# Down projections: 12 of 22 blocks as 2x2 block products by 7 half-size products instead of 8

## The chip, the cores and the metric

One core of a Trainium2 chip runs one layer of a decoder. The metric is the device time of one execution in microseconds, the median of several runs. The engines are named as in the profile: PE is TensorE (its weight loads are PEld), DVE is VectorE, ACT is ScalarE, POOL is GpSimd, and SP is SyncE, whose queue (SPq) issues the loads.

## The reference, cut to what matters

```python
def swiglu(x, w_gate, w_up, w_down):
    return (jax.nn.silu(x @ w_gate) * (x @ w_up)) @ w_down

x = x + 0.5 * rmsnorm(swiglu(rmsnorm(x, pre), w_gate, w_up, w_down), post)   # first FFN
x = x + rmsnorm(hybrid_mixer(rmsnorm(x, pre), ...), post)                     # attention and mLSTM
x = x + 0.5 * rmsnorm(swiglu(rmsnorm(x, pre), w_gate, w_up, w_down), post)   # second FFN
```

There are 512 tokens, the model is 1024 wide and the FFN 2816 wide, all in float32. The change lies in the last product of each FFN: the activations (512 x 2816) times `w_down` (2816 x 1024), called the down projection. The first FFN is named `a` in the tiles, the second `b`.

## The kernel before, in words

Float32 products are made of three PE products. Each operand is split into a high part in the PE's own format (a cast on ACT) and a low part (the operand minus its high part, a subtraction on DVE). A product is high x high + low x high + high x low.

The activations lie in SBUF as `aT`, 22 blocks of 128 FFN rows by 512 tokens. The down projection takes one block after the other. For each, `load_w` loads 128 rows of `w_down` (512 KB) into one of three `wf` buffers and splits them into `wh`, `wl` (128x1024, five buffers each), and `get_x` splits the block of `aT` into `ah`, `al` (128x512, five buffers each). Then `step` adds 24 matmuls of 512 columns: four tiles of 128 tokens, two halves of the 1024 columns, three products. The eight sums fill the eight PSUM banks. The last four blocks (`KEEP`) are held back and done tile by tile, so that the norm of one tile of tokens runs beside the matmuls of the next.

Ahead of the down projection, `seven` makes the gate and up products, one unit per block of FFN rows, already as 2x2 block products by seven. A unit has seven products of 12 matmuls of 256 columns; its seventh (`finish`) is put into the next unit. The seventh of the last unit is put behind the first half of the first block of the down projection (`bridge`), so that PE has work while DVE and ACT finish the unit. `qa` and `qb` are its banks, `z`, `uv`, `s` its small results.

What sets the order: DVE, ACT, PE and the load queue each work through their own list in order, as a scheduler wrote it when the kernel was built. In `seven`, the class `Order` ties each DVE or ACT instruction behind the one before it, so there the list is the code's order. A load waits for the last reader of the buffer that it fills. For a `wf` buffer that is the subtraction on DVE that makes the low part.

Of the kernel before, what the change touches and what calls it, by code (L numbers as in the profile page):

```python
# [10 lines left out]
F32 = mybir.dt.float32  # L11
F32R = mybir.dt.float32r
# [4 lines left out]
P = 128  # L17
T = 512
NT = T // P
D = 1024  # L20
KD = D // P
FF = 2816
NF = FF // P
# [9 lines left out]
WMAX = 1024  # L33
# [6 lines left out]
def tile_hybrid_block(ctx: ExitStack, tc: tile.TileContext, a: dict):  # L40
    nc = tc.nc

    ids = ctx.enter_context(tc.tile_pool(name="ids", bufs=1))
    wpool = ctx.enter_context(tc.tile_pool(name="wpool", bufs=1))
    hpool = ctx.enter_context(tc.tile_pool(name="hpool", bufs=1))
    const = ctx.enter_context(tc.tile_pool(name="const", bufs=1, side="right"))
    act = ctx.enter_context(tc.tile_pool(name="act", bufs=1, side="right"))

    def new_pool(name, side="right"):
        return tc.tile_pool(name=name, bufs=1, side=side, reuse_waits="tile")  # L50

    class Work:
        pool = None
# [4 lines left out]
    work = Work()  # L58
# [6 lines left out]
    def pair(name):  # L65
        return [bank(f"{name}_{b}") for b in range(2)]
# [127 lines left out]
        hTl = hpool.tile([P, KD, T], F32R, tag="hTl", name=f"hTl_{name}")  # L194
        return hTh, hTl

    def down(pool, n, chunk_src, get_x, post, finish, todo, name, bridge=None):
        pins = []
        accs = [None] * NT
        held = []  # L200
        for kk in range(n):
            xh, xl = get_x(kk)
            wh, wl = load_w(chunk_src(kk), f"{name}d{kk}")
            if kk < n - KEEP:
                for t in range(NT):
                    if kk == 0:
                        accs[t] = pair(f"acc_{name}{t}")
                    for b in range(2):
                        step(accs[t][b], xh, xl, wh, wl, t, b, kk == 0, False)
                    if bridge and kk == 0 and t == 1:  # L210
                        bridge()
# [12 lines left out]

    def step(out, xh, xl, wh, wl, t, b, first, last):
        tk = slice(t * P, (t + 1) * P)
        cs = slice(b * 512, (b + 1) * 512)
        nc.tensor.matmul(out, lhsT=xh[:, tk], rhs=wh[:, cs], start=first, stop=False)  # L228
        nc.tensor.matmul(out, lhsT=xl[:, tk], rhs=wh[:, cs], start=False, stop=False)  # L229
        nc.tensor.matmul(out, lhsT=xh[:, tk], rhs=wl[:, cs], start=False, stop=last)  # L230

    def flush(todo):
        return todo.pop(0)() if todo else None
# [1 line left out]
    Q = KD // 2 * P  # L235
    H = T // 2
    ADD, SUB, MUL = ALU.add, ALU.subtract, ALU.mult
# [39 lines left out]
        part(4)  # L277
        return parts

    def seven(fs, wgu, x, low, scr, aT, name):  # L280
        do = Order()
# [76 lines left out]
        for i in range(len(fs)):  # L358
            u, v, w = us[i:i + 3]
            u.open()  # L360
            if prev:
                prev.inner()
                prev.silu(1)
            u.product(u.a, 1, True, False)
# [12 lines left out]
            if prev:  # L377
                prev.finish()
            if v:
                low4 = v.take((4,), v.gu[1][:, 1:2, :], 1)  # L380
                low4()
            u.product(u.a, 2, False, True)
            u.silu(0)
            if v:
                v.take((7, 5), v.ab)()
            u.product(u.b, 7, False, False)
            u.product(u.c, 3, False, True)
            if w:
                w.front()
            prev = u  # L390
# [3 lines left out]

    PLAIN = 4

    def ffn(pool, todo, first_w, hT, wgu, wd, post, finish, name, begin=None, pins=()):
        hTh, hTl = hT
        aT = pool.tile([P, NF, T], F32, name=f"aT_{name}")
        st = ExitStack()  # L400
        low = st.enter_context(new_pool(f"parts_{name}", "left"))
        scr = st.enter_context(new_pool(f"gu_{name}"))

        def close(f, pg):
            s = scr.tile([P, 2, H], F32, tag="s", bufs=1, name=f"s_{name}{f}").rearrange("p a b -> p (a b)")
            nc.scalar.activation(s, pg[0], AF.Silu)
            nc.vector.tensor_tensor(aT[:, f, :], pg[1], s, op=MUL)

        def load_plain(f):
            return [load_w(wgu[f, :, b * 1024:(b + 1) * 1024], f"{name}gu{f}{b}",  # L410
                           after=pins if f < EARLY and f + b else ()) for b in range(2)]

        early = []
        for f in range(EARLY):
            w = first_w if first_w and f == 0 else load_plain(f)
            early.append((*w, pair(f"pg_{name}{f}")))
        by_halves([(pg, (wg, wu)) for wg, wu, pg in early], hTh, hTl, todo)
        for f in range(EARLY):
            close(f, early[f][2])
        x = None  # L420
        for f in range(EARLY, PLAIN):
            w = load_plain(f)
            if f == EARLY:
                x = token_parts(low, aT[:, NF - 16:, :], hTh, hTl, name)
            pg = pair(f"pg_{name}{f}")
            for b in range(2):
                ws(pg[b], w[b], KD, hTh, hTl)
            close(f, pg)
        last = seven(range(PLAIN, NF), wgu, x, low, scr, aT, name)

        dn = ExitStack()
        dlow = []

        def bridge():
            last()
            st.close()
            dlow.append(dn.enter_context(new_pool(f"low_{name}", "left")))
            work.pool = dn.enter_context(new_pool(f"dn_{name}"))
            if begin:
                begin()  # L440


        def get_x(kk):
            if kk == 0:
                ah, al = (wpool.tile([P, WMAX], F32R, tag=f"w{y}", bufs=5, name=f"a{y}_{name}{kk}")[:, :T] for y in "hl")
            else:
                ah, al = (dlow[0].tile([P, T], F32R, tag=f"a{y}", bufs=5, name=f"a{y}_{name}{kk}") for y in "hl")
            nc.scalar.copy(ah, aT[:, kk, :])
            nc.vector.tensor_tensor(al, aT[:, kk, :], ah.bitcast(F32), op=ALU.subtract)
            return ah, al  # L450

        pins = down(pool, NF, lambda kk: wd[kk], get_x, post, finish, todo, name, bridge)
        dn.close()
        return pins


    with new_pool("ffn_a") as fa:
# [28 lines left out]
        hT = []  # L486
# [8 lines left out]
            todo.append(lambda: turn_norm(t, h, *hT, "mx"))  # L495

        op_ctx.close()
        pins = ffn(fa, todo, first_w, hT1, a["wgu1"], a["wd1"], post1, finish1, "a", begin=load_gains)
    hTh, hTl = hT


# [482 lines left out]
    pins = down(mg, KD, lambda kk: a["wout"][kk], lambda kk: (meTh[:, kk, :], meTl[:, kk, :]), post2, finish2, todo, "o")  # L984
    gctx.close()
    mctx.close()

# [2 lines left out]
    with new_pool("ffn_b") as fb:  # L990
        def post3(t):
            return PostNorm(t, g_post2[0], [(work, "tmp"), (work, "tmp2")][t % 2], "f2", True)

        def finish3(t):
            for c in BANKS:
                nc.sync.dma_start(a["out"][t * P:(t + 1) * P, c], xs[t][:, c])

        ffn(fb, todo, None, hT2, a["wgu2"], a["wd2"], post3, finish3, "b",
            begin=lambda: g_post2.append(gain(a["ffn2_post_g"], "f2post")), pins=pins)


# [29 lines left out]
def _layout(inp):  # L1031
# [10 lines left out]
    r = {"x": np.asarray(inp["x"])[0]}  # L1042
    for i, n in ((1, "ffn1"), (2, "ffn2")):
        r[f"wgu{i}"] = np.concatenate([cols(f(f"{n}_w_gate")), cols(f(f"{n}_w_up"))], 2)
        r[f"wd{i}"] = f(f"{n}_w_down").reshape(NF, P, D)
# [43 lines left out]
```

## Time and profile before

| | us |
|---|---|
| median of 3 runs | 1371.52 (1370.53 to 1372.25) |
| the profiled execution | 1370.57 |
| its span, first to last instruction | 1368.8 |
| PE busy in the span | 1355.5 (99%) |
| PE weight loads | 1214.6 (89%) |
| DVE busy | 879.6 (64%) |
| ACT busy | 565.0 (41%) |

The first down projection runs from 239.46 to 362.6 us after the span's start, the second from 1241.04 to 1362.4. In a group of instructions the two numbers behind the bar are its busy time and the mean length of one in ns; matmuls overlap, so the length of one is more than the time from one start to the next. "Idle before" is time in which the engine stood still ahead of that group.

### The profile page before, as it was taken

What the parts mean: (1) busy time and instruction counts of PE and PEld (TensorE: products, weight loads), DVE (VectorE), ACT (ScalarE), POOL (GpSimd) and SP (SyncE); (2) the same over time, 40 slices, a digit from 0 to 9 for tenths busy, and PEclk for the clock granted to TensorE, in tenths of its full rate; (3) what the DMA queues carried; (4) which work ended last, traced back from release to release, by engine and by line L of the source; (5) the groups of instructions that cost most, each with busy time, mean ns of one, the idle gap of its engine ahead of it and who ended that gap; (6) DMA issues with size and microseconds to landing.
All of it is one profiled execution on the core that took longest, in us unless ns stands there. A gap on an engine that the chain in (4) does not pass through costs nothing.

```text
span 1368.8 us, 19779 instructions
## 1 busy us (share of the span) xinstructions
PE 1355.5 (99%) x8048; PEld 1214.6 (89%) x8048; DVE 879.6 (64%) x1370; ACT 565.0 (41%) x913; POOL 30.1 (2%) x52
## 2 busy tenths in 40 slices
PE   8999999999999999999999999999999999999998
PEld 7899999888899889888888888888888999998886
DVE  7799898433872885675756753333378889985333
ACT  5444444332633532435545443222264444444222
POOL 1000000000200000000000000000010000000000
PEclk9999999999999999999999999999999999999999
DMA  5333333523233222222222232223223233334221
GB/s 201 98 102 109 108 100 102 169 93 93 69 99 124 78 78 91 79 78 77 78 77 77 79 122 76 93 93 108 92 61 98 90 108 109 107 110 139 93 76 62
DMA packets 37371, 133.32 MB, mean 97 GB/s; under 512 B 4268, under 2 KB 4268, under 8 KB 37280
## 3 DMA queue, kind: packets, MB, share of 16 engines
q1 hardware_dynamic: 36144, 128.50, 29.1%
q0 software_dynamic: 1136, 3.56, 0.8%
q8 instruction: 63, 1.03, 0.3%
q14 instruction: 28, 0.23, 0.1%
HBM read 129.95 MB, written 2.10 MB: 96 GB/s over the span
## 4 chain that ended last, share of the span: by engine, by line
PE 98%; ACT 1%; DMA 1%; DVE 0%; issue 0%; SPq 0%; DVEq 0%; POOLq 0%; ACTq 0%
PE p L176 11%; PE qb_b L322 9%; PE qb_a L322 9%; PE pq L176 7%; PE pm L176 6%; PE qa_b L322 4%; PE qa_a L322 4%; PE acc_a L228 3%; PE acc_b L228 3%; PE acc_b L230 3%; PE acc_a L229 3%; PE acc_a L230 3%; PE acc_b L229 3%; PE pvo L810 2%; PE pvo L812 2%; PE pvo L811 2%
## 5 line engine op out<-in xcount | busy, mean ns | idle before, releaser
L228 PE MATMUL acc_a<-wh_ad,ah_a 128*128 128x512 f32 x176 | 68.7, 390 | 0.0
L229 PE MATMUL acc_a<-wh_ad,al_a 128*128 128x512 f32 x176 | 68.5, 389 | 0.0
L230 PE MATMUL acc_a<-wl_ad,ah_a 128*128 128x512 f32 x176 | 68.5, 389 | 0.0
L228 PE MATMUL acc_b<-wh_bd,ah_b 128*128 128x512 f32 x176 | 68.5, 389 | 0.0
L229 PE MATMUL acc_b<-wh_bd,al_b 128*128 128x512 f32 x176 | 68.5, 389 | 0.0
L230 PE MATMUL acc_b<-wl_bd,ah_b 128*128 128x512 f32 x176 | 68.5, 389 | 0.0
L88 DVE TENSOR_TENSOR wl_ad<-wf_ad,wh_ad 128x1024 fp32r<-128x1024 f32 x22 | 26.9, 1224 | 57.8 <-ACT wh_ad L86 57.8
L88 DVE TENSOR_TENSOR wl_bd<-wf_bd,wh_bd 128x1024 fp32r<-128x1024 f32 x22 | 26.9, 1224 | 57.8 <-ACT wh_bd L86 57.8
L176 PE MATMUL pq<-hTh_mx,wh_qk 128*128 128x512 f32 x160 | 63.2, 395 | 0.0
L176 PE MATMUL pq<-hTl_mx,wh_qk 128*128 128x512 f32 x160 | 62.4, 390 | 0.0
L88 DVE TENSOR_TENSOR wl_qk<-wf_qk,wh_qk 128x1024 fp32r<-128x1024 f32 x24 | 29.3, 1220 | 41.6 <-ACT wh_qk L86 31.3
L86 ACT CAST wh_ad<-wf_ad 128x1024 fp32r<-128x1024 f32 x22 | 22.9, 1048 | 69.7 <-PE acc_a L229 60.6
L86 ACT CAST wh_bd<-wf_bd 128x1024 fp32r<-128x1024 f32 x22 | 22.9, 1047 | 69.7 <-PE acc_b L229 60.6
L176 PE MATMUL pm<-hTh_mx,wh_mqk 128*128 128x512 f32 x128 | 50.3, 393 | 0.0
L810 PE MATMUL pvo<-wh_vo,hTh_mx 128*128 128x512 f32 x128 | 50.2, 392 | 0.0
L176 PE MATMUL pm<-hTl_mx,wh_mqk 128*128 128x512 f32 x128 | 49.9, 390 | 0.0
L176 PE MATMUL p<-hTh_mx,wh_gm 128*128 128x512 f32 x128 | 49.9, 390 | 0.0
L812 PE MATMUL pvo<-wl_vo,hTh_mx 128*128 128x512 f32 x128 | 49.8, 389 | 0.0
L176 PE MATMUL p<-hTl_mx,wh_gm 128*128 128x512 f32 x128 | 49.8, 389 | 0.0
L811 PE MATMUL pvo<-wh_vo,hTl_mx 128*128 128x512 f32 x128 | 49.8, 389 | 0.0
L86 ACT CAST wh_qk<-wf_qk 128x1024 fp32r<-128x1024 f32 x24 | 25.0, 1045 | 55.0 <-PE pw L558 28.8
L176 PE MATMUL pq<-hTh_mx,wl_qk 128*128 128x512 f32 x160 | 39.6, 389 | 0.0
(455 smaller groups left out, 4142.6 us busy)
## 6 DMA issues: line engine op xcount, KB each, us to landing
wf_qk<-in_wqk SPq DMA_DIRECT2D x24, 512.0 KB, 3.3
wf_ad<-in_wd SPq DMA_DIRECT2D x22, 512.0 KB, 3.4
wf_bd<-in_wd SPq DMA_DIRECT2D x22, 512.0 KB, 3.4
g_a<-in_wgu SPq DMA_DIRECT2D x18, 512.0 KB, 3.8
u_a<-in_wgu SPq DMA_DIRECT2D x18, 512.0 KB, 3.8
g_b<-in_wgu SPq DMA_DIRECT2D x18, 512.0 KB, 3.8
u_b<-in_wgu SPq DMA_DIRECT2D x18, 512.0 KB, 3.8
wf_mqk<-in_wmqk SPq DMA_DIRECT2D x16, 512.0 KB, 3.3
```

The costliest lines, as they stand in the source:

```text
L86: nc.scalar.copy(wh, wf)
L88: nc.vector.tensor_tensor(wl, wf, wh.bitcast(F32), op=ALU.subtract)
L176: nc.tensor.matmul(out, lhsT=wt[:, k * P:(k + 1) * P], rhs=x[:, k, tok], start=n == 0, stop=n == len(terms) - 1)
L228: nc.tensor.matmul(out, lhsT=xh[:, tk], rhs=wh[:, cs], start=first, stop=False)
L229: nc.tensor.matmul(out, lhsT=xl[:, tk], rhs=wh[:, cs], start=False, stop=False)
L230: nc.tensor.matmul(out, lhsT=xh[:, tk], rhs=wl[:, cs], start=False, stop=last)
L322: nc.tensor.matmul(out, lhsT=wt[:, i * P:(i + 1) * P], rhs=y[:, i, :], start=first and n == 0, stop=last and n == len(terms) - 1, skip_gro ...
L810: nc.tensor.matmul(out, lhsT=hTh[:, k, tk], rhs=wh[:, cs], start=k == 0, stop=False)
L811: nc.tensor.matmul(out, lhsT=hTl[:, k, tk], rhs=wh[:, cs], start=False, stop=False)
L812: nc.tensor.matmul(out, lhsT=hTh[:, k, tk], rhs=wl[:, cs], start=False, stop=k == KD - 1)
```

## The change

Twelve of the 22 blocks are taken together. Call A the activations cut into 2x2 parts (two halves of the tokens, two halves of six blocks), and B the rows of `w_down` cut likewise (two halves of six blocks, two halves of the columns). Eight part products become seven with sums of A's and B's parts, in the form of Winograd. Each of the seven has three steps (`g` = 0, 1, 2), each of two blocks and 12 matmuls of 512 columns. Steps are named by product and `g`: `20` is product 2, `g` = 0. Blocks 12 and 13 are done by halves of the tokens as steps `p0`, `p1`, `q0`, `q1` between and behind the others, and so their weights are loaded and split twice. That makes 25 steps in the order of the string `STEPS`. Blocks 14 to 21 go on as before, the last four held back.

The weights of the twelve blocks are loaded by parts (512 KB, two blocks by 512 columns) from a copy of `w_down` laid out for it on the host (`wdq`), into the same three `wf` buffers. In `run`, step n fetches for step n+3, makes the sums and casts for step n+2, and the low parts for step n+1. All DVE and ACT instructions of the 25 steps go through `Order`. `seven` gets a generator (`ahead`) and calls it in its last unit, so that the first splits are made there. Sums of products are made by DVE in the PSUM banks (`middle`, `late`).

```diff
+    HALF = 6
+    FILL = (12, 13)
+    STEPS = "20 21 10 50 60 11 51 61 12 52 62 22 p0 p1 70 30 71 31 72 32 40 41 42 q0 q1".split()
+    LOADS = {"1": ((0, 0),), "2": ((1, 0),), "5": ((0, 1),), "6": ((1, 1),), "7": ((1, 1), (0, 1)), "3": (),
+             "4": ((1, 0),)}
...
+        def fetch(self, s):
+            if s[0] in "pq":
+                t = act.tile([P, WMAX], F32, tag="wf", bufs=3, name=f"B{s}_{self.name}")
+                nc.sync.dma_start(t, self.wd[FILL[int(s[1])]])
...
+            for k, j in LOADS.get(s[0], ()):
+                t = act.tile([P, 2, T], F32, tag="wf", bufs=3, name=f"B{k}{j}_{self.name}{s}")
+                nc.sync.dma_start(t, halves(self.wdq[int(s[1]), k, j], T))
...
+            if k == "5":
+                self.tt(w, B(0, 1), B(0, 0), SUB)
+                self.tt(x, A(1, 0), A(1, 1), ADD)
+            elif k == "6":
+                self.tt(w, B(1, 1), self.t1, SUB)
+                self.tt(x, self.s1, A(0, 0), SUB)
+            elif k == "7":
+                self.tt(w, B(1, 1), B(0, 1), SUB)
+                self.tt(x, A(0, 0), A(1, 0), SUB)
+            elif k == "3":
+                self.tt(x, A(0, 1), halves(self.S[:, g, :], H), SUB)
+            elif k == "4":
+                self.tt(w, B(1, 0), w, SUB)
...
+        def product(self, s):
...
+            for i, o in enumerate(self.out[k]):
+                for m in range(2):
+                    tk, cs = slice(m * H + i * P, m * H + (i + 1) * P), slice(m * T, (m + 1) * T)
+                    for n, (x, w) in enumerate(((xh, wh), (xl, wh), (xh, wl))):
+                        nc.tensor.matmul(o, lhsT=x[:, tk], rhs=w[:, cs], start=k in "1256" and g + m + n == 0,
+                                         stop=False, skip_group_check=True)
...
+        def middle(self, s):
+            q1, p5 = self.S[:, 3:5, :], self.S[:, 5:7, :]
+            for i in range(2):
+                if s == "12":
+                    self.do("scalar", "copy", q1[:, i, :], self.out["1"][i])
+                elif s == "52":
+                    self.do("scalar", "copy", p5[:, i, :], self.out["5"][i])
+                elif s == "62":
+                    self.tt(self.out["6"][i], self.out["6"][i], q1[:, i, :], ADD)
+                elif s == "72":
+                    self.tt(self.out["1"][i], self.out["7"][i], p5[:, i, :], ADD)
+            if s == "62":
+                for i in range(2):
+                    self.tt(self.out["5"][i], self.out["6"][i], p5[:, i, :], ADD)
...
+            for n in range(3, len(STEPS)):
+                if n + 3 < len(STEPS):
+                    self.fetch(STEPS[n + 3])
+                if n + 2 < len(STEPS):
+                    self.sums(STEPS[n + 2])
+                    for x in "wx":
+                        self.cast(STEPS[n + 2], x)
+                if n + 1 < len(STEPS):
+                    for x in "wx":
+                        self.low(STEPS[n + 1], x)
+                self.product(STEPS[n])
+                self.middle(STEPS[n])
...
-        pins = down(pool, NF, lambda kk: wd[kk], get_x, post, finish, todo, name, bridge)
+        pins = down(NF, lambda kk: wd[kk], get_x, post, finish, todo, name, d.accs, d.after, d.late)
```

Three places show how the lists change; names are those of the first FFN with their buffer numbers. In them `B11_a70` is the loaded part B11 for step `70`, `T_a` and `S_a` hold the sums of weights and of activations, `wh`, `wl`, `xh`, `xl` with a step's name are the split operands, and `acca` to `accd` the banks of the four quarters of the result.

First DVE, before, from the last unit of `seven` into the down projection:

```order
L249 SCALAR_TENSOR_TENSOR aT_a_205<-z_a20_2612,s_a20_2613 128x512
L88 TENSOR_TENSOR wl_ad1_2902<-wf_ad1_2898,wh_ad1_2900 128x1024
L88 TENSOR_TENSOR wl_ad2_2936<-wf_ad2_2932,wh_ad2_2934 128x1024
L249 TENSOR_TENSOR z_a21_2729<-qb_a21_2726,uv_a21_2728 128x256 x2
L88 TENSOR_TENSOR wl_ad3_2970<-wf_ad3_2966,wh_ad3_2968 128x1024
L249 TENSOR_TENSOR z_a21_2729<-qb_a21_2726,q1_a21_2727 128x256
L249 SCALAR_TENSOR_TENSOR aT_a_205<-z_a21_2729,s_a21_2730 128x512
L449 TENSOR_TENSOR al_a1_2895<-aT_a_205,ah_a1_2894 128x512
```

And DVE now, in the middle of the 25 steps, from the low parts of `p0` to those of `30`:

```order
L247 TENSOR_TENSOR wlp0_a_3123<-Bp0_a_3096,whp0_a_3122 128x1024
L247 TENSOR_TENSOR xlp0_a_3126<-aT_a_205,xhp0_a_3125 128x256
L247 TENSOR_TENSOR T_a_2882<-B11_a70_3146,B01_a70_3148 128x1024
L247 TENSOR_TENSOR S_a_2883<-aT_a_205 128x512
L247 TENSOR_TENSOR wlp1_a_3151<-Bp1_a_3120,whp1_a_3150 128x1024
L247 TENSOR_TENSOR xlp1_a_3154<-aT_a_205,xhp1_a_3153 128x256
L247 TENSOR_TENSOR s4_a0_3196<-aT_a_205,S_a_2883 128x512
L247 TENSOR_TENSOR wl70_a_3173<-T_a_2882,wh70_a_3172 128x1024
L247 TENSOR_TENSOR xl70_a_3176<-S_a_2883,xh70_a_3175 128x512
L247 TENSOR_TENSOR T_a_2882<-B11_a71_3192,B01_a71_3194 128x1024
L247 TENSOR_TENSOR S_a_2883<-aT_a_205 128x512
L247 TENSOR_TENSOR wl30_a_3199<-B11_a70_3146,wh30_a_3198 128x1024
```

Where one subtraction of each size stood for 24 matmuls, now up to two of each size stand for 12, and the sums of step `70` stand ahead of the low parts of `p1`.

Second the load queue (SP), before, at the start of the down projection:

```order
L293 DMA u_a21_2521<-in_wgu1 128x1024
L81 DMA wf_ad0_2830<-in_wd1 128x1024
L81 DMA wf_ad1_2898<-in_wd1 128x1024
L81 DMA wf_ad2_2932<-in_wd1 128x1024
L81 DMA wf_ad3_2966<-in_wd1 128x1024
```

And now, in the middle of the 25 steps:

```order
L429 DMA Bp0_a_3096<-in_wd1 128x1024
L429 DMA Bp1_a_3120<-in_wd1 128x1024
L433 DMA B11_a70_3146<-in_wdq1 128x1024
L433 DMA B01_a70_3148<-in_wdq1 128x1024
L433 DMA B11_a71_3192<-in_wdq1 128x1024
L433 DMA B01_a71_3194<-in_wdq1 128x1024
L433 DMA B11_a72_3240<-in_wdq1 128x1024
L433 DMA B01_a72_3242<-in_wdq1 128x1024
```

Steps of product 7 take two loads each and those of product 3 none. By the buffers that the build gave them, `B01_a70` goes where `Bp0_a` was and waits for `wlp0_a`; `B01_a71` goes where `Bp1_a` was and waits for `wlp1_a`; `B01_a72` goes where `B11_a70` was and waits for `wl30_a`.

Third PE, before, at the start of the first block:

```order
L228 MATMUL acc_a0_0_2836<-wh_ad0_2832,ah_a0_2826 128x512
L229 MATMUL acc_a0_0_2836<-wh_ad0_2832,al_a0_2827 128x512
L230 MATMUL acc_a0_0_2836<-wl_ad0_2834,ah_a0_2826 128x512
L228 MATMUL acc_a0_1_2837<-wh_ad0_2832,ah_a0_2826 128x512
L229 MATMUL acc_a0_1_2837<-wh_ad0_2832,al_a0_2827 128x512
```

And now, from the end of `p1`'s first four matmuls to `70`'s:

```order
L227 MATMUL accc_a1_2863<-whp1_a_3150,xhp1_a_3153 128x512
L497 MATMUL accb_a2_2864<-wh70_a_3172,xh70_a_3175 128x512
L497 MATMUL accb_a3_2865<-wh70_a_3172,xh70_a_3175 128x512
L227 MATMUL acca_a0_2858<-whp1_a_3150,xlp1_a_3154 128x512
L227 MATMUL acca_a0_2858<-wlp1_a_3151,xhp1_a_3153 128x512
L227 MATMUL acca_a1_2859<-whp1_a_3150,xlp1_a_3154 128x512
```

The scheduler put the first two matmuls of `70`, which need the casts of its sums, ahead of the matmuls of `p1` that need low parts. In the whole program PE has 72 matmuls of 512 columns fewer.

More of the change, by code (lines that the diff above doesn't have):

```diff
@@ L195, in new_hT, with down @@
         return hTh, hTl
-    def down(pool, n, chunk_src, get_x, post, finish, todo, name, bridge=None):
+    def down(n, chunk_src, get_x, post, finish, todo, name, accs=None, first=0, late=lambda: None):
         pins = []
-        accs = [None] * NT
         held = []
-        for kk in range(n):
+        accs = accs or [pair(f"acc_{name}{t}") for t in range(NT)]
+        for kk in range(first, n):
             xh, xl = get_x(kk)
@@ L205, in down @@
                 for t in range(NT):
-                    if kk == 0:
-                        accs[t] = pair(f"acc_{name}{t}")
                     for b in range(2):
                         step(accs[t][b], xh, xl, wh, wl, t, b, kk == 0, False)
-                    if bridge and kk == 0 and t == 1:
-                        bridge()
+                    if kk == first and t == 1:
+                        late()
             else:
@@ L227, in step @@
         cs = slice(b * 512, (b + 1) * 512)
-        nc.tensor.matmul(out, lhsT=xh[:, tk], rhs=wh[:, cs], start=first, stop=False)
-        nc.tensor.matmul(out, lhsT=xl[:, tk], rhs=wh[:, cs], start=False, stop=False)
-        nc.tensor.matmul(out, lhsT=xh[:, tk], rhs=wl[:, cs], start=False, stop=last)
+        for n, (x, w) in enumerate(((xh, wh), (xl, wh), (xh, wl))):
+            nc.tensor.matmul(out, lhsT=x[:, tk], rhs=w[:, cs], start=first and n == 0, stop=last and n == 2,
+                             skip_group_check=True)
     def flush(todo):
@@ L278, in token_parts, with seven @@
         return parts
-    def seven(fs, wgu, x, low, scr, aT, name):
-        do = Order()
+    def seven(do, fs, wgu, x, low, scr, aT, name, ahead):
         tt = lambda out, p, q, op: do("vector", "tensor_tensor", out, p, q, op=op)
@@ L363, in seven @@
                 prev.silu(1)
+            if not v:
+                next(ahead)
             u.product(u.a, 1, True, False)
@@ L385, in seven @@
                 v.take((7, 5), v.ab)()
+            else:
+                next(ahead)
             u.product(u.b, 7, False, False)
@@ L398, in ffn @@
+    def ffn(pool, todo, first_w, hT, wgu, wdq, wd, post, finish, name, begin=None, pins=()):
         hTh, hTl = hT
         aT = pool.tile([P, NF, T], F32, name=f"aT_{name}")
-        st = ExitStack()
+        st, sr = ExitStack(), ExitStack()
         low = st.enter_context(new_pool(f"parts_{name}", "left"))
-        scr = st.enter_context(new_pool(f"gu_{name}"))
+        scr = sr.enter_context(new_pool(f"gu_{name}"))
         def close(f, pg):
@@ L428, in ffn @@
             close(f, pg)
-        last = seven(range(PLAIN, NF), wgu, x, low, scr, aT, name)
+        do = Order()
+        d = Down(do, wdq, wd, aT, scr, name)
+        ahead = d.run()
+        last = seven(do, range(PLAIN, NF), wgu, x, low, scr, aT, name, ahead)
         dn = ExitStack()
[L432 to L440, printed above, removed]
+        next(ahead)
+        last()
+        st.close()
+        d.xp = dn.enter_context(new_pool(f"low_{name}", "left"))
+        next(ahead)
+        sr.close()
+        work.pool = dn.enter_context(new_pool(f"dn_{name}"))
+        if begin:
+            begin()
+        for _ in ahead:
+            pass
         def get_x(kk):
[L444 to L447, printed above, removed]
+            ah, al = (d.xp.tile([P, T], F32R, tag=f"x{y}", bufs=5, name=f"a{y}_{name}{kk}") for y in "hl")
             nc.scalar.copy(ah, aT[:, kk, :])
@@ L497, in tile_hybrid_block @@
         op_ctx.close()
-        pins = ffn(fa, todo, first_w, hT1, a["wgu1"], a["wd1"], post1, finish1, "a", begin=load_gains)
+        pins = ffn(fa, todo, first_w, hT1, a["wgu1"], a["wdq1"], a["wd1"], post1, finish1, "a", begin=load_gains)
     hTh, hTl = hT
@@ L982, in finish2 @@
         todo.append(lambda: turn_norm(t, h, *hT2, "f2"))
-    pins = down(mg, KD, lambda kk: a["wout"][kk], lambda kk: (meTh[:, kk, :], meTl[:, kk, :]), post2, finish2, todo, "o")
+    pins = down(KD, lambda kk: a["wout"][kk], lambda kk: (meTh[:, kk, :], meTl[:, kk, :]), post2, finish2, todo, "o")
     gctx.close()
@@ L1044, in _layout @@
         r[f"wgu{i}"] = np.concatenate([cols(f(f"{n}_w_gate")), cols(f(f"{n}_w_up"))], 2)
-        r[f"wd{i}"] = f(f"{n}_w_down").reshape(NF, P, D)
+        wd = f(f"{n}_w_down").reshape(NF, P, D)
+        r[f"wd{i}"] = wd
+        r[f"wdq{i}"] = wd[:12].reshape(2, 3, 2, P, 2, 512).transpose(1, 0, 4, 3, 2, 5).reshape(3, 2, 2, P, 1024)
         r[f"{n}_pre_g"], r[f"{n}_post_g"] = f(f"{n}_pre_g"), f(f"{n}_post_g")
```

101 lines of the change are left out of this document (99 added, 2 removed).

## Prediction

> **What bounds the kernel now.** I read the page first: busy times, the chain that ended last, and the groups of the down projection.
>
> ```profile
> PE 1355.5 (99%) x8048; PEld 1214.6 (89%) x8048; DVE 879.6 (64%) x1370; ACT 565.0 (41%) x913; POOL 30.1 (2%) x52
> PE 98%; ACT 1%; DMA 1%; DVE 0%; issue 0%; SPq 0%; DVEq 0%; POOLq 0%; ACTq 0%
> L228 PE MATMUL acc_a<-wh_ad,ah_a 128*128 128x512 f32 x176 | 68.7, 390 | 0.0
> ```
>
> PE is the chain, and it stood still 0.0 us ahead of the down projection's matmuls. So each matmul removed is worth its spacing, as long as PE does not begin to wait. The 390 ns in the group is the length of one; the spacing is read from the timeline, where one `step` is three matmuls:
>
> ```profile
> 245.03 0.39 PE L228 MATMUL acc_a<-wh_ad,ah_a 128*128 128x512 f32 x1
> 340.91 0.39 PE L228 MATMUL acc_a<-wh_ad,ah_a 128*128 128x512 f32 x1
> 238.98 0.64 PE L322 MATMUL qb_a<-hTh_f,wl_a 128*128 128x256 f32 x4
> ```
>
> Between the first two lie 141 triples: 95.88 / 423 = 0.2267 us a matmul. The third row gives 0.12 us for one of 256 columns (0.64 for four, of which the last is 0.28 long). The second question is who would bind if PE had less to do, by stretches of the timeline: `seven` of the first FFN, then its down projection.
>
> ```profile
> 61.07:242.50 181.43, 181.43 (x1503) 180.94 (x1503) 157.11 (x224) 86.26 (x129) 0.00 (x0) 1.00 0.33 103
> 242.50:360.00 117.50, 117.50 (x533) 97.67 (x533) 50.53 (x69) 39.36 (x65) 4.02 (x7) 1.00 0.31 102
> ```
>
> The fourth number is DVE: 87% busy in `seven` without ever holding PE up, 43% in the down projection. That room is what the change spends.
>
> **The change part by part. Matmuls.** Twelve blocks are 12 x 24 = 288 matmuls; 21 steps of 12 are 252. The filled blocks 12 and 13 stay at 48. Gone are 36 per FFN, 72 in all: 36 x 0.2267 = 8.16 us per FFN, 16.3 us in all. By the page's 390 ns it would be 28 us, but that time overlaps with the next matmul. [...]
>
> **DVE's work.** Its prices are spacings between starts on a busy DVE.
>
> ```profile
> 213.28 0.68 DVE L249 TENSOR_TENSOR ab_a<-u_a 128x512 f32<-128x512 f32 x1
> 213.88 0.68 DVE L249 TENSOR_TENSOR uv_a<-qb_a,q_a 128x512 f32<-128x512 f32 x1
> 214.48 1.22 DVE L249 TENSOR_TENSOR wl_a<-cd_a,wh_a 128x1024 fp32r<-128x1024 f32 x1
> 215.62 0.42 DVE L249 TENSOR_TENSOR z_a<-qb_a,q_a 128x256 f32<-128x256 f32 x1
> 219.50 0.75 DVE L249 TENSOR_TENSOR z_a<-qb_a,uv_a 128x256 f32<-128x256 f32 x2
> 220.18 1.22 DVE L249 TENSOR_TENSOR wl_a<-g_a,wh_a 128x1024 fp32r<-128x1024 f32 x1
> ```
>
> So 0.60 us for 512 columns, 1.14 for 1024, 0.34 for 256. The second row reads a PSUM bank and costs the same. No row shows DVE writing a PSUM bank; the nearest are that one (0.60) and the dearest 512-column row of DVE, below, at a length of 0.75. I take 0.60, since reading from PSUM changes nothing, and keep 0.75 for the range.
>
> ```profile
> L170 DVE SCALAR_TENSOR_TENSOR x<-fg_f,r_pf,x 128x512 f32<-128x512 f32 x6 | 4.2, 747 | 0.3
> ```
>
> One step is 12 x 0.2267 = 2.72 us of PE. Its low parts cost DVE 1.14 + 0.60 = 1.74, and steps of products 5, 6 and 7 need a sum of each size too, another 1.74: 3.48 us of DVE for 2.72 of PE. So DVE falls behind in `50 60 51 61 52 62` and `70 71 72` and catches up only in steps without sums. I count from PE's first matmul of step `20` (239.46 in the trace) to step `40`, whose third matmul needs `xl40`; behind it only `42` and the cheap `q0`, `q1` are left.
>
> DVE in that stretch, along its new list: 1024 columns: 19 low parts (`10` to `40` less `20`, `21`), ten sums of weights and `t1`, 30 x 1.14 = 34.2. 512 columns: 18 low parts, nine sums for products 5 and 6 and 7, three for 3, six sums in PSUM, and one of `seven`, 37 x 0.60 = 22.2. 256 columns: 5 x 0.34 = 1.7. Together 58.1 us.
>
> PE in it: 20 steps of 2.72 = 54.4, the last product of `seven` 12 x 0.12 = 1.44, two matmuls of `40` 0.45. Together 56.3 us. Without any wait DVE is 1.8 us late at `40`.
>
> **DVE's waits.** The loads: three `wf` buffers, and each load waits for a low part on DVE.
>
> ```profile
> 252.93 1.23 DVE L88 TENSOR_TENSOR wl_ad<-wf_ad,wh_ad 128x1024 fp32r<-128x1024 f32 x1 [2.58 <-ACT wh_ad L86]
> 254.18 0.33 SPq L81 DMA_DIRECT2D wf_ad<-in_wd  x1
> wf_qk<-in_wqk SPq DMA_DIRECT2D x24, 512.0 KB, 3.3
> wf_ad<-in_wd SPq DMA_DIRECT2D x22, 512.0 KB, 3.4
> DMA to landing us min/median/max: 3.2/3.4/5.0
> g_a<-in_wgu SPq DMA_DIRECT2D x18, 512.0 KB, 3.8
> 2.12 7.37 DMA wf_agu<-in_wgu
> 9.49 0.02 issue
> 9.51 1.05 ACT wh_agu L86
> ```
>
> A load is issued 0.02 us after the subtraction ends and the reader starts 0.02 after the landing. The parts lie in one piece in memory as `wqk` and `wd` do (3.3, 3.4), not in rows of a wider array as `wgu` (3.8); I take 3.3, with 3.2 and 3.8 to 5.0 as ends. From the start of the subtraction that frees the buffer to its reader's start the way is 1.22 + 3.34 = 4.56 us; what DVE has to do between is all that hides it:
> - `B01_a70` waits for `wlp0`; behind it stands only `xlp0`: 1.14 + 0.34. DVE waits 3.1 us.
> - `B01_a71` waits for `wlp1`; `xlp1`, `s4`, `wl70`, `xl70` follow: 1.14 + 0.34 + 0.60 + 1.14 + 0.60 = 3.82. It waits 0.7.
> - `B01_a72` waits for `wl30`; `xl30`, `s4`, `wl71`, `xl71`: 4.08, and some 0.1 more since `s4` overwrites what `xl30` read. It waits 0.4.
>
> Behind each of them the load queue itself stands still; the next entry, `B11` of the next `7`, waits for `T70` or `T71` anyway. All other loads have over 4.6 us of DVE work between. The second wait for a cast on ACT or for PE. At the start the casts of `21` and `10` stand behind ACT's silu, which stands behind `z`:
>
> ```profile
> 239.97 0.75 DVE L249 TENSOR_TENSOR z_a<-qb_a,uv_a 128x256 f32<-128x256 f32 x2
> 240.75 0.42 ACT L249 ACTIVATE s_a<-z_a 128x256 f32<-128x256 f32 x1 [0.51 <-DVE z_a L249]
> 227.24 1.04 ACT L249 CAST wh_a<-ab_a 128x1024 fp32r<-128x1024 f32 x1
> 228.17 0.62 ACT L448 CAST ah_a<-aT_a 128x512 fp32r<-128x512 f32 x1
> ```
>
> From the end of `z` to the end of a 512 cast: 0.03 + 0.32 + 0.62 = 1.0 us, then a 1024 cast behind it (0.52 + 1.04 - 0.62, against 0.60 on DVE): 0.3 more. Ahead of `wl60`, the cast begins as its sum ends and takes 1.04, with 0.5 us of DVE work beside it: 0.5. The four sums in PSUM wait for PE to end `62`: 0.7. With 4.2 for the loads, DVE waits 7.2 us.
>
> **The sum.** DVE reaches `xl40` at 58.1 + 7.2 = 65.3, PE could have been there at 56.3: PE stands still 9.0 us, and 0.2 more ahead of `xl41` (`T42`, `wl41`, `xl41` are 2.9 us against 2.72). The saving is 8.2. Each FFN is 1.0 us longer, 2.0 in all; some ten restarts of PE per FFN, each with its weight load in the open (0.11 us before the transpose's start in the chain's rows at 18.32, against 0.04 where the weights were there), add about 0.3 each, most of it beside DVE's lag:
>
> ```profile
> 18.32 0.11 issue
> 12.03 0.04 issue
> ```
>
> So 2.0 + 0.5 = +2.5 us. The profiled execution of 1370.57 would become 1373.1; the median of the runs stands 0.95 above it, so 1374.0.
>
> Edits at nothing: ACT has 21 x (0.93 + 0.52) and a few smaller, some 38 us for 68 of PE. `late` and the low parts of the eight plain blocks are 15 us of DVE beside 43 of PE; if that cover went, up to 1.2. The eleven more loads per FFN need 512 KB in 2.72 us, 193 GB/s, while
>
> ```profile
> 2.00:6.00 4.00, 3.84 (x25) 2.74 (x23) 0.15 (x1) 1.17 (x3) 0.31 (x1) 1.00 0.96 354
> ```
>
> shows 354 GB/s. The norms, the mixer and `seven`'s other 17 units keep their lists.
>
> **The rivals.**
> 1. PE stays the bound (the other side: faster). If the loads were there in time and no cast late, DVE's 58.1 would pass PE's 56.3 by 1.8 us only: 2 x (1.8 - 8.2) = -12.8, or -16.3 if that hid too. For it: `seven` ran with DVE 87% busy and no wait of PE. Against: `B01_a70` is freed by the last instruction but one ahead of its reader. It decides where DVE's lag falls under 8.2 us. 1355 to 1359.
> 2. Only part of the waits come: a load at 3.2 and the casts of the start done earlier, 2 us less per FFN. Gives 1370 or, with 3 less, 1368.
> 3. Slow loads. 3.8 to 4.4 as `g_a` or the slowest plain ones: three waits of 0.5 to 1.1 more per FFN, +3 to +6.6: 1377 to 1381. For it: two loads in flight at once, twice the traffic. Against: 354 GB/s above.
> 4. PE's clock falls in its longest gap, some 3 us ahead of `70`. The trace has no such gap at speed; its longest are
>
> ```profile
> 9.90 1.23 PE L148 MATMUL pt_f<-ident,h_f 128*128 128x128 f32 x8 [1.50 <-DVE h_f L140]
> 6.00:10.00 4.00, 1.32 (x9) 0.97 (x10) 2.56 (x5) 1.64 (x3) 0.80 (x2) 1.00 1.00 340
> ```
>
> 1.50 us, with the clock at 1.00. If it fell to half for as long as the gap, 3 us of matmuls would take 3 more; DVE's lag hides some. 0 to +3 per FFN: up to 1380. [...]
>
> **How the numbers follow.** A measurement of this kernel can tell about 0.2%, 2.7 us. The likeliest, DVE as the bound with the waits above, has 0.52, between 1369 and 1379: DVE's prices to 2% (1.2 us per FFN), PSUM sums at 0.75 (+0.9 per FFN), the loads at 3.2 to 3.5. Rival 1 has 0.06, 2 has 0.17, 3 has 0.17, 4 has 0.08. The range 1366 to 1381 leaves out rival 1 and the ends of 3 and 4. Faster: rival 1, most of 2, the low end of the likeliest, 0.22. Slower (over 1374.3): 3, 4 and nearly half of the likeliest, 0.46. Within 0.2%: 0.32.
>
> **What would show it.** Right: 72 matmuls fewer; in the down projections PE idle some 9 us each, ended by DVE's `T70` or ACT's cast of it, by `xl` and `wl` of `71`, `72` and `40`; one gap near 3 us; DVE above 90% busy in the first 70 us; the chain that ended last showing DVE and ACT there; all other stages as long as before. Wrong: PE idle under 5 us per FFN (rival 1 or 2), landings over 3.6 (3), matmuls spaced wider than 0.23 or a lower clock (4), or a different length of `seven` or of the mixer.

## The result and the profile after

The changed kernel took 1381.12 us (median of four runs, 1379.73 to 1382.26), beside 1371.03 for the kernel before: a ratio of 1.0072, 95% interval 1.0055 to 1.009. That is 10 us slower, where the forecast was 2.5 us; it lies at the very end of the forecast's range (1366 to 1381) and above the 1369 to 1379 of its likeliest case. A second set of five runs gave 1380.19 against 1371.52, 1.0066 (1.0053 to 1.0079). The profiled execution took 1381.4 with a span of 1379.6, against 1368.8 before.

The page of the changed kernel, busy times and the chain that ended last:

```profile
PE 1353.3 (98%) x7976; PEld 1203.3 (87%) x7976; DVE 967.5 (70%) x1478; ACT 600.1 (43%) x965; POOL 30.1 (2%) x52
PE 90%; DVE 5%; DMA 2%; ACT 1%; issue 1%; POOL 0%; SPq 0%; DVEq 0%; POOLq 0%; ACTq 0%
```

72 matmuls are gone (8048 to 7976). A chain that was 98% PE now has 5% of DVE, 2% of loads and 1% of ACT. The stretches of the timeline say where (the columns are length, then PE, PEld, DVE, ACT and POOL busy with their counts, then the granted clock, DMA's share, GB/s):

```profile
61.07:242.50 181.43, 181.43 (x1503) 180.94 (x1503) 156.77 (x224) 82.87 (x125) 0.00 (x0) 1.00 0.33 102
242.50:360.00 117.50, 110.62 (x465) 87.30 (x465) 90.42 (x114) 56.95 (x86) 2.92 (x5) 0.97 0.49 152
239.57:309.13 69.56, 62.74 (x256) 47.84 (x254) 59.14 (x73) 33.23 (x46) 1.26 (x2) 0.95 0.55 168
```

`seven` is as before. In the second stretch DVE went from 50.5 to 90.4 us and PE fell from 117.5 to 110.6. The third is the part that the prediction summed, from PE's first matmul of step `20` to the low part that step `40` waits for. The length of a down projection I take from the start of its first matmul to that of its last. Before, it was 122.75 us (239.46 to 362.21) and 120.94. After, it is 128.14, by these two rows, and 125.86 in the second FFN:

```profile
239.57 0.40 PE L497 MATMUL acca_a<-wh_a,xh_a 128*128 128x512 f32 x1
...
367.71 0.39 PE L227 MATMUL accd_a<-wl_ad,ah_a 128*128 128x512 f32 x1
```

That is 5.39 + 4.92 = 10.3 of the 10.8 us by which the span grew; the rest of the program is 0.5 longer.

DVE's part of the timeline shows the three waits that the prediction had named, before the sum `T` of 70, 71 and 72, and the end of the counted stretch (`xl40`). The number in brackets is the idle time ahead, with what ended it:

```profile
276.19 0.42 DVE L247 TENSOR_TENSOR xlp_a<-aT_a,xhp_a 128x256 fp32r<-128x256 f32 x1
279.92 1.23 DVE L247 TENSOR_TENSOR T_a<-B_a,B_a 128x1024 f32<-128x1024 f32 x1 [3.31 <-DMA B_a<-in_wdq]
...
287.49 1.23 DVE L247 TENSOR_TENSOR T_a<-B_a,B_a 128x1024 f32<-128x1024 f32 x1 [1.93 <-DMA B_a<-in_wdq]
...
295.25 1.23 DVE L247 TENSOR_TENSOR T_a<-B_a,B_a 128x1024 f32<-128x1024 f32 x1 [1.73 <-DMA B_a<-in_wdq]
...
308.44 0.69 DVE L247 TENSOR_TENSOR xl_a<-aT_a,xh_a 128x512 fp32r<-128x512 f32 x1
```

They come to 6.97 us; the prediction had 3.1 + 0.7 + 0.4 = 4.2. The chain that ended last runs through the same three loads (start, length):

```profile
276.30 3.59 DMA B_a<-in_wdq
...
282.91 4.46 DMA B_a<-in_wdq
...
290.48 4.65 DMA B_a<-in_wdq
```

And here is PE over the gap ahead of 70 and the one ahead of 72:

```profile
279.06 0.61 PE L227 MATMUL accc_a<-whp_a,xhp_a 128*128 128x512 f32 x2
282.85 1.22 PE L497 MATMUL accb_a<-wh_a,xh_a 128*128 128x512 f32 x2 [3.17 <-ACT xh_a L247]
283.87 0.63 PE L227 MATMUL acca_a<-whp_a,xlp_a 128*128 128x512 f32 x1
284.29 0.63 PE L227 MATMUL acca_a<-wlp_a,xhp_a 128*128 128x512 f32 x1
...
298.21 0.73 PE L497 MATMUL accb_a<-wh_a,xh_a 128*128 128x512 f32 x2 [1.75 <-ACT xh_a L247]
...
299.67 0.56 PE L497 MATMUL accc_a<-wh_a,xl_a 128*128 128x512 f32 x1
300.03 0.63 PE L497 MATMUL accc_a<-wl_a,xh_a 128*128 128x512 f32 x1
...
302.59 0.63 PE L497 MATMUL accc_a<-wh_a,xh_a 128*128 128x512 f32 x1
303.02 0.46 PE L497 MATMUL accb_a<-wh_a,xl_a 128*128 128x512 f32 x1
303.32 0.40 PE L497 MATMUL accb_a<-wl_a,xh_a 128*128 128x512 f32 x1
```

Behind both gaps, matmuls start 0.43 us apart instead of 0.23: half the clock, for some 3.4 us each time. The granted clock of these two stretches (the third number from the end) is 0.50:

```profile
282.67:286.08 3.41, 3.23 (x8) 2.56 (x9) 2.89 (x5) 1.70 (x3) 0.00 (x0) 0.50 0.79 262
299.74:303.15 3.41, 3.41 (x10) 2.63 (x9) 3.41 (x4) 1.16 (x2) 0.00 (x0) 0.50 0.41 141
```

That was rival 4. So two causes lay in the trace at once, slower loads and a slower clock, and the experiments had to tell them apart: theory A, that DVE with its waits sets the time and the slow matmuls lie in a lag that is there anyway; theory B, that the slow matmuls and the restarts are what was missed.

### The profile page after: what moved, and what is told of

It reads as the page before. It is cut to its first block, busy times and chain, and to the rows that moved or that the text cites. A ratio compares the mean times of both kernels' runs of the same rounds, so it can differ in the third digit from the quotient of the medians.

```text
span 1379.6 us, 19883 instructions
## 1 busy us (share of the span) xinstructions
PE 1353.3 (98%) x7976; PEld 1203.3 (87%) x7976; DVE 967.5 (70%) x1478; ACT 600.1 (43%) x965; POOL 30.1 (2%) x52
## 4 chain that ended last, share of the span: by engine, by line
PE 90%; DVE 5%; DMA 2%; ACT 1%; issue 1%; POOL 0%; SPq 0%; DVEq 0%; POOLq 0%; ACTq 0%
PE p L176 11%; PE qb_b L319 9%; PE qb_a L319 9%; PE pq L176 7%; PE pm L176 6%; PE qa_b L319 4%; PE qa_a L319 4%; PE pvo L982 2%; PE pvo L984 2%; PE pvo L983 2%; PE acc_o L227 2%; PE pg_a L186 2%; PE pg_b L186 2%; PE pq L186 2%; PE pg_a L176 2%; PE pg_b L176 2%
## 5 line engine op out<-in xcount | busy, mean ns | idle before, releaser
L1135 DVE SCALAR_TENSOR_TENSOR t<-t,p 128x512 f32<-128x512 f32 x16 | 11.0, 688 | 42.7 <-PE p L176 42.7
L88 DVE TENSOR_TENSOR wl_mqk<-wf_mqk,wh_mqk 128x1024 fp32r<-128x1024 f32 x16 | 19.6, 1223 | 29.6 <-ACT wh_mqk L86 25.3
L873 DVE SCALAR_TENSOR_TENSOR z<-pm,cw,z 128x511 f32<-128x511 f32 (+2 forms) x48 | 35.3, 744 | 1.4 <-ACT z L871 0.9
L319 PE MATMUL qa_a<-hTl_f,wh_a 128*128 128x256 f32 x144 | 36.1, 283 | 0.0
L319 PE MATMUL qa_b<-hTl_f,wh_b 128*128 128x256 f32 x144 | 36.1, 283 | 0.0
L319 PE MATMUL qa_a<-hTh_f,wh_a 128*128 128x256 f32 x144 | 36.1, 283 | 0.0
L319 PE MATMUL qa_b<-hTh_f,wh_b 128*128 128x256 f32 x144 | 36.1, 283 | 0.0
L247 ACT CAST wh_a<-cd_a 128x1024 fp32r<-128x1024 f32 x18 | 18.9, 1051 | 38.9 <-DVE cd_a L247 38.9
L176 PEld LDWEIGHTS pq<-hTh_mx,wl_qk 128*128 128x128 f32 x160 | 30.0, 188 | 6.2
L247 ACT CAST wh_b<-cd_b 128x1024 fp32r<-128x1024 f32 x18 | 18.9, 1051 | 38.0 <-DVE cd_b L247 38.0
```

Source lines behind the costliest of these rows:

```text
L88: nc.vector.tensor_tensor(wl, wf, wh.bitcast(F32), op=ALU.subtract)
L176: nc.tensor.matmul(out, lhsT=wt[:, k * P:(k + 1) * P], rhs=x[:, k, tok], start=n == 0, stop=n == len(terms) - 1)
L247: self.last[eng] = getattr(getattr(nc, eng), fn)(*args, **kw).ins
L319: nc.tensor.matmul(out, lhsT=wt[:, i * P:(i + 1) * P], rhs=y[:, i, :], start=first and n == 0, stop=last and n == len(terms) - 1, skip_gro ...
L873: nc.vector.scalar_tensor_tensor(z[:, s:], src[:, :T - s], cw[:, ct, 3 - s:4 - s], z[:, s:], op0=ALU.mult, op1=ALU.add)
L1135: nc.vector.scalar_tensor_tensor(t1[:, b, :], t1[:, b, :], 1.0, p2[b], op0=ALU.add, op1=ALU.mult)
```

## The experiments

**Own buffers for B01.** The loads of part B01 get two buffers of their own, so that they no longer wait for a low part of `p0`, `p1` or `30`.

```diff
-                t = act.tile([P, 2, T], F32, tag="wf", bufs=3, ...)
+                pool, tag, n = (self.xp, "wf7", 2) if self.xp and (k, j) == (0, 1) else (act, "wf", 3)
+                t = pool.tile([P, 2, T], F32, tag=tag, bufs=n, ...)
```

> The loads of part B01 (products 5 and 7) get two buffers of their own, so that none of them waits for a low part of a fill step; nothing else is changed. Theory A (DVE is the bound, and its waits for the loads B01 of 70, 71 and 72, 3.31 + 1.93 + 1.73 = 7.0 us per down projection in the trace of the changed kernel, are the excess): both FFNs get some 6.5 to 7 us shorter, 1367 to 1368 us, and the three waits are gone from DVE's list. Theory B (PE's clock at half rate after its gaps and the restarts are the excess; the loads only fill a lag that DVE's work has anyway): 3 to 6 us less in all, 1375 to 1378 us. Theory C (the loads are late because the queue moves too much, wherever they lie): the waits reappear at other loads, 1379 to 1381 us.

1366.39 us, ratio to the kernel before 0.996 (0.9948 to 0.9973): some 14 us less than the changed kernel, and faster than the kernel before. Its timeline of DVE at the first two of the three places (the sum `T` follows with no idle time):

```profile
276.13 0.42 DVE L247 TENSOR_TENSOR xlp_a<-aT_a,xhp_a 128x256 fp32r<-128x256 f32 x1
276.47 1.22 DVE L247 TENSOR_TENSOR T_a<-B_a,B_a 128x1024 f32<-128x1024 f32 x1
...
281.42 0.69 DVE L247 TENSOR_TENSOR xl_a<-S_a,xh_a 128x512 fp32r<-128x512 f32 x1
282.02 1.22 DVE L247 TENSOR_TENSOR T_a<-B_a,B_a 128x1024 f32<-128x1024 f32 x1
```

The down projections are 119.99 and 118.15 us long, 8.15 and 7.71 less. Theory A had 6.5 to 7 each, a little less than came off; the time is 8.6 us under the low end of theory B, and C's waits didn't come back. But this edit also took away PE's gaps, and with them the slow clock (0.998 granted over the profiled span, as in the kernel before, where the changed kernel had 0.995); the next experiment keeps the waits.

**PE kept busy.** Matmuls by a zero tile fill PE's long gaps.

```diff
+    IDLE = {"p1": 15, "30": 4, "31": 7}
...
+            for i in range(IDLE.get(s, 0)):
+                with tc.issue_after(self.mm):
+                    self.mm = nc.tensor.matmul(self.accs[0][0], lhsT=self.zero[:, :P], rhs=self.zero,
+                                               start=False, stop=False, skip_group_check=True).ins
```

> The changed kernel with matmuls by a zero tile added in PE's three long gaps (15 ahead of p1, 4 ahead of 30, 7 ahead of 31 in each down projection, 0.23 us each, on a bank to which zero is added); waits and loads stay. Theory A: PE's clock stays at 1.00, but PE only waits longer for DVE behind it; 1379.5 to 1382 us, at most 1.5 us less than the changed kernel. Theory B: the two stretches per down projection with matmuls 0.43 us apart disappear and with them 1.6 to 2.6 us each, 1373 to 1376 us.

1378.92 us, 1.0055 (1.0042 to 1.0068), between the two theories. I ran it again beside the changed kernel itself:

> The changed kernel once more, unaltered, on the chip of the next three: 1380 to 1382 us.

> The kernel with the zero matmuls in PE's gaps once more, beside the changed kernel on the same chip. Theory A (DVE sets the end of the steps, the half-rate stretches lie in PE's lag): 0 to 1.5 us under the changed kernel. Theory B (they add to the time): 3 us or more under it. The earlier run stood 2.2 us under a time of the changed kernel from another chip, between the two.

1380.19 for the changed kernel and 1378.52 for this one, 1.7 us apart, again between. In this kernel the clock holds: it is granted 1.00 over both down projections in both profiles. In the first gap, the zero matmuls stand ahead of `p1` (the last five of the 15 are shown), and the first matmul of 70 behind them is 0.39 us long, not 0.63:

```profile
281.75 1.29 PE L492 MATMUL acca_a<-zero_a 128*128 128x512 f32 x5
282.88 0.62 PE L227 MATMUL acca_a<-whp_a,xhp_a 128*128 128x512 f32 x2
283.33 0.62 PE L227 MATMUL accc_a<-whp_a,xhp_a 128*128 128x512 f32 x2
283.79 0.39 PE L504 MATMUL accb_a<-wh_a,xh_a 128*128 128x512 f32 x1
```

The medians don't decide, but the profiles do, once DVE's waits for loads are set beside the lengths. The list of DVE's waits for this kernel has (total, times, longest)

```profile
DVE T_a L247 <- DMA B_a<-in_wdq: 7.0, 3, 3.3
DVE T_b L247 <- DMA B_b<-in_wdq: 7.4, 3, 3.6
```

in the changed kernel and

```profile
DVE T_a L248 <- DMA B_a<-in_wdq: 6.1, 3, 3.0
```

in this one. Read so for the five profiles in which the steps stand in the order of the changed kernel and the sums are made:

| kernel | first: length, waits for loads, difference | second: the same |
|---|---|---|
| changed | 128.14, 7.0, 121.1 | 125.86, 7.4, 118.5 |
| changed, again | 127.02, 6.8, 120.2 | 125.26, 6.8, 118.5 |
| PE kept busy | 126.34, 6.1, 120.2 | 124.56, 6.1, 118.5 |
| PE kept busy, again | 125.94, 5.7, 120.2 | 124.61, 6.2, 118.4 |
| own buffers | 119.99, 0, 120.0 | 118.15, 0, 118.2 |

In nine of ten down projections the length is one number for each FFN (120.0 to 120.2 in the first, 118.2 to 118.5 in the second) plus the waits for loads, whether PE's clock fell (the two rows of the changed kernel) or not. The tenth is 0.9 us longer. In it the slow stretch lies at 299.7 to 303.2, right ahead of the sums of banks that wait for PE to end 72. In the run "changed, again" the first FFN has no slow stretch there, and the same two sums (the last row) wait for nothing:

```profile
304.43 0.70 DVE L247 TENSOR_TENSOR accd_a<-accb_a,S_a 128x512 f32<-128x512 f32 x1 [0.28 <-PE accb_a L497]
305.57 0.70 DVE L247 TENSOR_TENSOR accd_a<-accb_a,S_a 128x512 f32<-128x512 f32 x1 [0.43 <-PE accb_a L497]
```

```profile
304.34 1.29 DVE L247 TENSOR_TENSOR accd_a<-accb_a,S_a 128x512 f32<-128x512 f32 x2
```

So theory A holds: the slow clock cost 0.9 us once (0.7 of it in these two waits), and elsewhere nothing that these profiles can tell. The 1.7 to 2.2 us between the medians are in the profiles a load time, 0.6 to 1.3 us less wait per down projection in the kernel with the zero tile. Why its loads are shorter is open (last section).

**Fill steps laid between.** Buffers as in the changed kernel, but three blocks in halves, and the fill steps between the others.

```diff
-    FILL = (12, 13)
-    STEPS = "... 22 p0 p1 70 30 71 31 72 32 40 41 42 q0 q1".split()
+    FILL = (12, 13, 14)
+    STEPS = "... 22 p0 p1 70 30 71 31 p2 72 32 q0 40 q1 41 q2 42".split()
```

> The changed kernel with block 14 as a third one in halves and the fill steps laid between the others: ... 22 p0 p1 70 30 71 31 p2 72 32 q0 40 q1 41 q2 42; buffers as in the changed kernel. Theory A: the loads wait for the same kind of low parts, DVE stays late, PE's fill work only moves its waits: 2 to 3 us less in all, 1378 to 1380 us. A rival (PE stands still only because a step with sums stands behind another; work laid between would hide DVE's lag, waits for loads too): 8 us less or more, 1373 us or under.

1380.48 us, 1.0061 (1.0047 to 1.0075): no gain that can be told from the changed kernel's times, where theory A had 2 to 3 us and the rival 8. The loads still wait for low parts just ahead of their readers. That of B01 for 72 now waits for the low part of 31, not of 30, and DVE's wait for it grew from 1.73 to 3.25 us. Two waits more came ahead of the sums for 41 and 42, so that all five come to 9.8 us (10.1 in the second FFN):

```profile
298.64 1.22 DVE L247 TENSOR_TENSOR T_a<-B_a,B_a 128x1024 f32<-128x1024 f32 x1 [3.25 <-DMA B_a<-in_wdq]
```

```profile
DVE T_a L247 <- DMA B_a<-in_wdq: 9.8, 5, 3.5
```

The order does hide something: the down projections are 126.32 and 126.49 us long, and without these waits 116.5 and 116.4, 2 to 4 us less than in the table. The longer waits take it back.

**No sums ahead of the products.** First with own buffers and `p0`, `p1` between the products 7, then as the only edit to the changed kernel.

```diff
             if k == "5":
-                self.t1, self.s1 = w, x
-                self.tt(w, B(0, 1), B(0, 0), SUB)
-                self.tt(x, A(1, 0), A(1, 1), ADD)
+                x, w = A(1, 0), B(0, 1)
 ...             (likewise for 6, 7, 3 and 4)
```

> The sums ahead of the products are left out (each product takes a plain part of the weights and of the tokens), with the own buffers and with p0 and p1 laid between the products 7; loads, casts, low parts, matmuls and the sums of banks stay. DVE's list is some 20 us shorter, so PE should be the bound, and the time shows what the 72 matmuls are worth. By their spacing of 0.2267 us, 16.3 us less than before, and some 2 us back for restarts and the start: 1356 to 1359 us. If a matmul less is worth less than its spacing here: over 1362 us.

> The changed kernel with the sums ahead of the products left out and nothing else: its own order, its three buffers, its loads for 7 behind the low parts of p0 and p1. Theory A (the loads are late because DVE frees their buffers late; with 20 us less on DVE per down projection they are there in time): no wait of DVE for B01, PE without a wait, 1354 to 1357 us. A rival (three buffers are too few for these loads, whatever DVE does): PE waits 3 us or more ahead of 70, 1361 us or more.

Both kernels leave out part of the computation, so that their results are not the layer's; only their times are of use here. They took 1354.89 us, 0.9878 (0.9865 to 0.9892), a little under the forecast of 1356 to 1359, and 1355.16, 0.988 (0.9866 to 0.9893), as forecast. In the second, three buffers, two loads for each 7 and the order of the steps are those of the changed kernel, and yet PE stands still nowhere in the stretch:

```profile
239.55:310.00 70.45, 70.45 (x319) 58.55 (x318) 51.55 (x63) 42.43 (x59) 1.26 (x2) 1.00 0.64 204
```

The loads land later than ever (median 4.5 us between 270 and 305 us), but they are issued early enough, because DVE is ahead of PE; now DVE waits for PE:

```profile
291.56 0.70 DVE L247 TENSOR_TENSOR accd_a<-accb_a,S_a 128x512 f32<-128x512 f32 x1 [2.67 <-PE accb_a L483]
```

So buffers and loads are not too few by themselves: the loads are late because DVE frees the buffers late. And the matmuls are worth what was counted: the down projections are 114.61 and 112.81 us (114.67 and 112.78 in the second), 8.1 us each less than before, where 36 x 0.2267 = 8.16.

**Both, own buffers and the fill between.**

> Own buffers for B01 and the fill steps laid between the others, both: 22 p0 p1 70 30 71 31 p2 72 32 q0 40 q1 41 q2 42. With own buffers alone (1366.4 us) DVE was still 5.4 us later per down projection than PE's work alone would be. Theory A: the third fill step and the two q steps, with 1.5 us of DVE for 2.7 of PE, take up most of it; 1358 to 1361 us, and faster than both kernels. If the order of the fill steps is worth as little as it was without the own buffers (0.6 us): 1365 to 1366 us.

1362.45 us, 0.9934 (0.9921 to 0.9946): 9 us faster than the kernel before, the best kernel with the full computation. The order that gained 0.6 us at most alone gains some 4 once the loads of B01 wait for no low part. The forecast of 1358 to 1361 is missed by 1.5 us: the waits for loads before the sums for 41 and 42 came with the order,

```profile
DVE T_a L247 <- DMA B_a<-in_wdq: 1.2, 2, 0.7
```

and 0.9 us for the sums of banks that wait for 72. It stands 7.3 to 7.6 us above the kernels without sums, about what DVE's sums may still cost.

## Why the forecast had the sign and missed the size

- **Matmuls.** 8.16 us per FFN: 8.14 and 8.13 in the first kernel without sums. The spacing of 0.2267 us was the right price.
- **DVE's work, 58.1 us.** The counted stretch took 69.56 us, of which DVE waited 6.97 for loads, 1.84 for casts and 1.50 for sums of banks. That leaves 59.25. Some 0.08 us are lost at each of ten waits, because a wait begins at an instruction's end and the spacing in the sum is that much shorter than the length; with that it is 58.4. The list and its prices held. (DVE was busy for 85% of this stretch, 59.14 of 69.56 us, not for the 90% that the prediction named as a sign: the waits were longer.) A sum written into PSUM costs DVE 0.61, as this row and the next start (273.86) show; the price for the range, 0.75, wasn't needed:

```profile
273.25 0.70 DVE L247 TENSOR_TENSOR accb_a<-accb_a,S_a 128x512 f32<-128x512 f32 x1 [0.43 <-PE accb_a L497]
273.86 1.29 DVE L247 TENSOR_TENSOR accc_a<-accb_a,S_a 128x512 f32<-128x512 f32 x2
```

- **The loads: the term that failed.** 4.2 us forecast, 7.0 and 7.4 measured. The places, the waited-for buffers and the order were right, and the first wait was right to 0.2 us. The other two were 0.7 and 0.4 forecast and 1.93 and 1.73 measured, since the loads took 4.46 and 4.65 us instead of 3.34. The queue shows how they differ from the first: the load of B11, freed by the sum before, is issued 1.74 us ahead of that of B01 and is still under way.

```profile
281.17 0.33 SPq L433 DMA_DIRECT2D B_a<-in_wdq  x1
...
282.91 0.33 SPq L433 DMA_DIRECT2D B_a<-in_wdq  x1
```

  The prediction had said that B11 waits for that very sum, and then took for B01 the price of a load alone. It gave two loads in flight as rival 3 (3.8 to 4.4 us a load, 1377 to 1381 us, a chance of 0.17) and argued against it with 354 GB/s of moved bytes, which is a rate and says nothing of one load's landing. In the whole profile of the changed kernel, 30 such loads of 512 KB (of `wdq`, `wd` and `wqk`) that had the queue to themselves took 3.5 to 4.4 us, 3.6 in the median; the 13 that were issued 1.2 to 2 us behind a single one under way took 4.1 to 4.8, 4.6 in the median. The profile before had six of the second kind, at the start of its two down projections (1.1 to 1.8 us behind another): they took 3.9 to 5.0 us, and the price could have been read there. Rival 3 is what came, with loads slower still: 2.8 us in the first FFN and 3.2 in the second, 6.0 of the 7.1 us that were missed. The prediction's sign for it, landings over 3.6 us, came too: the median of `B_a` is 3.7.
- **Sums of banks.** 0.7 us forecast for those after 62; they took 0.79. The two after 72, which the sum left out, took 0.71 more in this FFN; in the second FFN and in the repeat's first they waited for nothing, so this is not a missing term but the slow clock ahead of them (the 0.9 us above).
- **Casts.** 1.0 + 0.3 + 0.5 = 1.8 forecast, 0.99 + 0.25 + 0.60 = 1.84 measured. The terms of the prediction's waits come to 6.7, not to the 7.2 that it wrote; the slip lay on the right side by chance.
- **PE's idle time.** Forecast 9.2 us; by the profile's waits 6.7, with the rest of the lag spent on matmuls at half clock and on restarts. DVE set the time either way. The restart at 0.3 us each was right in size (298.21 to 298.87 is 0.66 us for two matmuls of 0.2267, and the third takes 0.34), but by luck: the two rows that it was taken from, 0.11 and 0.04 us, differ by 0.07 only.
- **Rival 4**, the clock, came in the trace (0.50 granted) but cost 0.9 us in one of the two down projections; it was not the reason. **Rival 1**, PE stays the bound, would have needed more than the loads in time: with the waits for loads gone, a down projection is still 5.4 us longer than PE's work (119.99 against 114.61), where rival 1 had 1.8.

## What to carry to other kernels

A saving on the bound engine is worth only what the next engine's list, with its waits, leaves of it; add up that list in time order and look for every load whose buffer is freed by an instruction just ahead of the load's reader. There a microsecond of landing time is a microsecond of the kernel, and the price is that of a load behind another one (4.6 us here, where one alone took 3.6) if one was issued one or two microseconds before. Mend the waits first: here the fill work laid between them gained nothing in the end until the loads of B01 had buffers of their own, since longer waits took back what it hid.

## What the runs showed of the hardware

**The clock fell behind some of PE's gaps and held behind others, and the length of the gap doesn't tell which.** In the first profile of the changed kernel the spacings (0.36 at 299.67, 0.30 at 303.02, 0.43 between) put the slow stretch at about 299.75 to 303.18, 3.4 us. The granted clock is 0.50 from 299.74 to 303.15, and in this profile's down projections in two more stretches: 3.41 us (282.67 to 286.08) and 6.83 us (1289.60 to 1296.43). The gap of 1.75 us that ends at 298.21 was enough for the first, and gaps of 3.17 and 3.47 us end at 282.85 and 1290.43. In the second FFN of the same profile there is a gap of 1.64 us too (1304.30 to 1305.94), and the clock held. In the changed kernel run again, a gap of 3.22 us changed nothing and one of 2.12 did. The second fence has the granted clock where the first gap ends and behind the second:

```profile
1289.53 0.74 PE L497 MATMUL accb_b<-wh_b,xh_b 128*128 128x512 f32 x2 [3.22 <-ACT xh_b L247]
...
1297.02 0.73 PE L497 MATMUL accb_b<-wh_b,xh_b 128*128 128x512 f32 x2 [2.12 <-ACT xh_b L247]
```

```profile
1287.96:1291.37 3.41, 1.84 (x8) 1.50 (x9) 3.41 (x5) 3.08 (x4) 0.00 (x0) 1.00 0.62 196
1298.20:1301.61 3.41, 3.41 (x9) 2.64 (x9) 1.89 (x3) 0.62 (x1) 0.00 (x0) 0.50 0.50 159
```

The slow stretch there runs from 1298.20 to 1301.61. In the down projections of three profiles (the changed kernel, the same again, the fill steps laid between) the clock fell in or behind eight gaps, of 1.75, 1.81, 2.12, 3.17, 3.29, 3.36, 3.38 and 3.47 us; it held behind those of 1.77, 1.88 and 3.22 us and behind all of 1.64 us or less. So the same gap can cost PE nothing, or half the clock for 3.4 us. In two down projections it was longer: the 6.83 us above, and in the second with the fill steps laid between, where matmuls were about 0.43 us apart from 1288.37 to 1294.09. No run set the gaps on purpose, and what decides is not shown.

**A 512 KB load has a different time in different programs.** The loads of `wqk` lie in the mixer, which no edit touches. In the median they took 3.3 us in the kernel before, 3.7 in both profiles of the changed kernel, 3.6 or 3.7 with own buffers, fill between or no sums, and 3.2 and 3.3 in the two with the zero tile. The first row is of the changed kernel's page, the second of the kernel with PE kept busy:

```profile
wf_qk<-in_wqk SPq DMA_DIRECT2D x24, 512.0 KB, 3.7
```

```profile
wf_qk<-in_wqk SPq DMA_DIRECT2D x24, 512.0 KB, 3.2
```

It looks like a property of the built program: the two programs that were profiled twice agree with themselves to 0.1 us, the one with the zero tile from two chips, while different programs on one chip do not (3.2 with the zero tile, 3.6 with own buffers). What in the program makes the difference was not tried. A landing time taken from the kernel before was off by up to 0.4 us here, and three loads hung on it.
